# A hybrid HGRN2 / ConvFFN trunk: the order of the prologue written out, two more scale blocks on TensorE, and 32 bytes more of constants

## The chip, the cores and the metric

The kernel runs on one core of a Trainium2 chip. The metric is the time of one execution on the device in microseconds (us), the median of several runs. Beside the runs there is one profiled execution, of which every row below is taken. Engines are named as in the profile: PE is TensorE (PEld its weight loads), DVE VectorE, ACT ScalarE, POOL GpSimd, SP the queue that issues the transfers.

## The reference, cut to what matters

`DEPTH` is 1, so one layer runs: an HGRN2 mixer (8 heads, 2048 latent tokens behind 256 context tokens, width 1024) and a gated ConvFFN. What the change touches is the way into the mixer:

```python
m_l = (silu(c) @ w_ada + b_ada)          # six vectors of 1024: shift, scale, gate, ...
m_c = silu(c_ctx) @ w_ada + b_ada        # the same for the context tokens
hl = rmsnorm(lat, norm_g) * (1.0 + sc1) + sh1
hc = rmsnorm(cx,  norm_g) * (1.0 + csc1) + csh1
q, zf_fwd, zf_bwd, v, g = split(h @ w_in, 5)
f = lb + (1.0 - lb) * sigmoid(zf)        # forward and backward gates of the scan
```

`lb` comes from a softmax over two rows of logits.

## The kernel before

Everything runs with features on the partitions. The 2304 tokens are cut into units of 384 columns (`UN`), three token tiles each; the first unit holds the two context tiles and the first latent tile. For each unit a `Hidden` object makes the normed and modulated activations: `load` (one transfer to `xT`), `squares` (ACT, two halves), `sums` (four adds over the eight feature blocks), `scales` (a PE sum over partitions into `zs`, `rms_scale` with a power on POOL, a diagonal `dg`), `spread` (a PE matmul of `dg` with ones into `zr`, and two multiplications of `xT` by it on DVE), then per feature block k `high(k)` (ACT: scale and shift, then a rounded copy `hh`) and `low(k)` (DVE: the rest `hl = xT - hh`). A product is made of three fp32r matmuls, high by high, high by low and low by high (lines 337, 338, 339 for the first unit's gates; 488, 489, 490 elsewhere).

Before the loop over heads and units there is the prologue, `begin`. It makes SiLU(c), copies it along the partitions as rows `silrow` (a diagonal `dgs`, four PE matmuls, four ACT copies), and for each of the eight feature blocks j loads two blocks of `w_ada`: one for the shift and one for the scale. `by_pe(j, i)` multiplies a block with SiLU(c) on PE (eight fp32 matmuls; the trace shows each as two). For j under `NPE` = 3 the scale block goes that way too; for the others `by_dve(j)` makes two dot products on DVE (`junk`, line 320). The factors `B1` (shift) and `A1` (scale) were made on DVE, lines 327 and 328. `split_w0(ty)` rounds one 512 KB type of the first head's weights (`wh` or `vh`, ACT) and makes its rest (`wl` or `vl`). `gates(k)` adds feature block k to the first unit's two gate sums. Meanwhile the second unit's activations are begun; its sums, and the rest of one weight type, ran on POOL (`sums(pool)`, `split_w0(4, pool)`).

`begin` was recorded like all else, and the tile framework's scheduler set the order on each engine: it could also pull later work into the prologue, such as the products of the first unit's values (the 24 matmuls `z<-vh,hh` of 384 columns, lines 488 to 490) and the second unit's `high` and `low`. From then on the first unit goes on with `unit` (lines 523 and following), and the second unit's gates begin with the `z<-hh,wh` matmul behind the two transposes of line 656.

Constants lie at the bottom of the on-chip memory: `vec`, `ident`, `mhalf` (8 columns of -0.5, 32 bytes per partition), `ones` and so on; pools stacked on the left side follow them, other pools hang from the right side.

Of the kernel before, what the change touches and what calls it, by code (L numbers as in the profile page):

```python
# [9 lines left out]
F32 = mybir.dt.float32  # L10
# [3 lines left out]
AF = mybir.ActivationFunctionType  # L14
OP = mybir.AluOpType
# [4 lines left out]
D = 1024  # L20
# [3 lines left out]
KT = 8  # L24
# [18 lines left out]
UN = 384  # L43
NSC = 3
NS = 12
SEG = 33
NPE = 3


def body(ctx, tc, a, out):  # L50
# [18 lines left out]
    def small(name, shape=(128, 8), dt=F32):  # L69
        return cst.tile(list(shape), dt, name=name)  # L70

    mhalf = small("mhalf")
    pool.memset(mhalf, -0.5)

    def rms_scale(dst, ss, n, width):

        dve.tensor_scalar(dst, ss, 1.0 / width, EPS, OP.mult, OP.add)
        pool.tensor_tensor(dst, dst, mhalf[:, 0:n], OP.pow)
# [69 lines left out]
    class Hidden:  # L148
# [15 lines left out]
                ks = slice(g * 4, g * 4 + 4)  # L164
                act.activation(self.sq[:, ks], self.x[:, ks], AF.Square)

        def sums(self, e=dve):
            q = self.sq
            for i, j, n in ((0, 2, 2), (4, 6, 2), (0, 4, 2), (0, 1, 1)):
                e.tensor_tensor(q[:, i:i + n], q[:, i:i + n], q[:, j:j + n], OP.add)  # L170

        def scales(self):
            z = self.ps.tile([128, NSC, 2], F32, name="zs", tag="tr")
            for s in range(NSC):
                pe.matmul(z[:, s], self.sq[:, 0, s * 128:(s + 1) * 128], ones[:, 0:2],
                          start=True, stop=True)
            rs = self.xp.tile([128, NSC], F32, name="rsx", tag="rsx", bufs=2)
            rms_scale(rs, z[:, :, 0], NSC, D)
            self.dg = self.xp.tile([128, NSC, 128], F32, name="dg", tag="dg")
            diag(self.dg, rs)  # L180

        def spread(self):
            z = self.ps.tile([128, 1, UN], F32, name="zr", tag="tr")
            pe.matmul(z[:, 0], ones, self.dg.rearrange("p s n -> p (s n)"), start=True, stop=True)
            for g in range(2):
                x = self.x[:, g * 4:g * 4 + 4]
                dve.tensor_tensor(x, x, z.to_broadcast([128, 4, UN]), OP.mult)

        def modulate(self, k):
            for m, c in ((1, slice(0, self.nc)), (0, slice(self.nc, UN))):  # L190
# [19 lines left out]

        def steps(self):
            return [lambda: (self.load(), self.squares()), self.sums, self.scales,
                    self.spread] + self.pairs()

    def diag(dst, w):
        n = w.shape[-1]
# [26 lines left out]
    def begin(xp, ps):  # L243


        p0 = pool_(c0, "p0", side="right")
        act.activation(sil, vec[:, V_C:V_C + 16], AF.Sigmoid)
        dve.tensor_tensor(sil, sil, vec[:, V_C:V_C + 16], OP.mult)
        silv = sil.rearrange("p (two k) -> p k two", two=2)

        hid = [Hidden(u, u, xp, ps, x) for u, x in
               enumerate((place(5, [128, KT, UN], F32, "xT"), place(4, [128, KT, UN], F32, "xT"),
                          None))]
        w = head_tiles()
# [12 lines left out]
        def split_w0(ty, e=dve):
            wh, wl = type_parts(w, ty)
            raw = raws[ty].rearrange("p (k n) -> p k n", k=KT)
            act.activation(wh, raw, AF.Copy)  # L270
            e.tensor_tensor(wl, raw, wh.bitcast(F32), OP.subtract)

        hid[0].load()
        piece(0)
        piece(1)
        raw_w(1, 2)
        piece(2)
        hid[1].load()
        piece(3)
        piece(4)  # L280
        raw_w(0, 3, 4)
        for j in range(5, KT):
            piece(j)

        l0, l1 = vec[:, V_LB:V_LB + 16], vec[:, V_LB + 16:V_LB + 32]
        mx = p0.tile([128, 16], F32, name="mx")
        e2 = p0.tile([128, 2, 16], F32, name="e2")
        eb = p0.tile([128, 32], F32, name="eb")
        pool.memset(eb, float(np.e))
        bp = p0.tile([128, 8], F32, name="bp")  # L290
        acc = p0.tile([128, 2, 8], F32, name="dot")

        dgs = place(2, [128, 16, 128], F32, "dgs")
        silrow = xp.tile([128, 2, D], F32, name="silrow", tag="xT")
        for q in range(4):
            qs = slice(q * 4, q * 4 + 4)
            diag(dgs[:, qs], sil[:, qs])
            z = ps.tile([128, 512], F32, name="z", tag="sc", bufs=2)
            pe.matmul(z, ones, dgs[:, qs].rearrange("p s n -> p (s n)"), start=True, stop=True)
            act.activation(silrow[:, q // 2, q % 2 * 512:(q % 2 + 1) * 512], z, AF.Copy)  # L300
        dve.tensor_tensor(mx, l0, l1, OP.max)
        dve.tensor_tensor(e2[:, 0], l0, mx, OP.subtract)
        dve.tensor_tensor(e2[:, 1], l1, mx, OP.subtract)
        e2f = e2.rearrange("p a b -> p (a b)")
        pool.tensor_tensor(e2f, eb, e2f, OP.pow)
        dve.tensor_scalar(bp, vec[:, V_BA + 8:V_BA + 16], 1.0, None, OP.add)

        def by_pe(j, i):
            z = ps.tile([128, 2, 64], F32, name="z", tag="sc", bufs=2)
            b = blocks.pop((j, i)).rearrange("p (k n) -> p k n", k=KT)  # L310
            for k in range(KT):
                pe.matmul(z, b[:, k], silv[:, k, :, None].to_broadcast([128, 2, 64]),
                          start=k == 0, stop=k == KT - 1)
            return z[:, :, 0]

        def by_dve(j):
            b = blocks.pop((j, 1))
            for m in range(2):
                junk = xp.tile([128, D], F32, name="junk", tag="acc")
                dve.scalar_tensor_tensor(junk, b, 1.0, silrow[:, m], OP.mult, OP.mult,  # L320
                                         accum_out=acc[:, m, j:j + 1])
            return acc[:, :, j]

        def ada(j):
            shift = by_pe(j, 0)
            scale = by_pe(j, 1) if j < NPE else by_dve(j)
            dve.tensor_scalar(B1[:, :, j], shift, vec[:, V_BA + j:V_BA + j + 1], None, OP.add)
            dve.tensor_scalar(A1[:, :, j], scale, bp[:, j:j + 1], vec[:, V_NG + j:V_NG + j + 1],
                              OP.add, OP.mult)

        zs = [ps.tile([128, UN], F32, name="z", tag="pj", bufs=3) for _ in range(2)]

        def gates(k):
            h, l = part("h", 0)[:, k], part("l", 0)[:, k]
            for d in range(2):
                sh, sl = w[0][d]
                pe.matmul(zs[d], sh[:, k], h, start=k == 0, stop=False)
                pe.matmul(zs[d], sh[:, k], l, start=False, stop=False)
                pe.matmul(zs[d], sl[:, k], h, start=False, stop=k == KT - 1)

        high = lambda k: hid[0].high(slice(k, k + 1))
        low = lambda k: hid[0].low(slice(k, k + 1))

        hid[0].squares()
        hid[0].sums()
        dve.tensor_tensor(mx, e2[:, 0], e2[:, 1], OP.add)
        dve.reciprocal(mx, mx)
        dve.tensor_tensor(lb, e2[:, 0], mx, OP.mult)
        dve.tensor_tensor(oml, e2[:, 1], mx, OP.mult)
        ada(0)  # L350
        ada(1)
        hid[0].scales()
        split_w0(1)
        hid[0].spread()
        split_w0(2)
        high(0)
        high(1)
        low(0)
        ada(2)
        high(2)  # L360
        low(1)
        gates(0)
        ada(3)
        high(3)
        low(2)
        gates(1)
        hid[1].squares()
        hid[1].sums(pool)
        ada(4)
        high(4)  # L370
        low(3)
        gates(2)
        ada(5)
        high(5)
        low(4)
        gates(3)
        split_w0(0)
        split_w0(3)
        gates(4)
        ada(6)  # L380
        high(6)
        low(5)
        split_w0(4, pool)
        hid[1].scales()
        gates(5)
        ada(7)
        high(7)
        low(6)
        hid[1].spread()
        low(7)  # L390
        gates(6)
        gates(7)
# [27 lines left out]
    def mixer_scan():  # L420
        xp = pool_(c1, "xp", side="right")
        ps = pool_(c1, "ps", space=PSUM)
        head0, begun, hid = begin(xp, ps)
        c0.close()
        gp = pool_(c1, "gp", side="right")

# [1121 lines left out]
```

## Time and profile before

| what | value |
|---|---|
| three runs | 2859.32, 2859.48, 2864.54 us; median 2859.48 |
| the profiled execution | 2864.76 us, its span 2863.0 us, so 1.8 us lie outside of the span |
| PE busy | 2802.6 us, 98% of the span |
| DVE, ACT, POOL busy | 2093.5, 1151.4 and 610.4 us |
| mean granted TensorE clock | 0.992 |

How to read the rows: a timeline row gives the start (us), the duration (us), engine, line, operation, out<-in, shapes, how many were merged, and in brackets the idle time before and what ended it. A row of the windows gives for each stretch its length, then busy time and count by engine, the granted clock, the share of the transfer engines and GB/s. A row of the chain gives start, length, engine, tile and line.

### The profile page before, as it was taken

How to read it: one execution, taken by the hardware profiler on the slowest of the kernel's cores; microseconds unless marked ns; L12 is line 12 of the kernel's file. 1: busy time of each engine (PE TensorE's matmuls, PEld its weight loads, DVE VectorE, ACT ScalarE, POOL GpSimd, SP SyncE). 2: the span in 40 equal slices, each digit the busy share in tenths (PEclk: the TensorE clock that was granted, in tenths of full speed). 3: DMA queues.
4: the chain of work that ended last, by engine and by line, in shares of the span. 5: the costliest groups of instructions: out<-in, count | busy, mean ns of one | idle time of the engine just before them, and what ended most of it. 6: DMA issues, size and time to landing. Idle time of an engine off the chain costs nothing.

```text
span 2863.0 us, 42888 instructions
## 1 busy us (share of the span) xinstructions
PE 2802.6 (98%) x15768; PEld 2484.1 (87%) x15768; DVE 2093.5 (73%) x3486; ACT 1151.4 (40%) x2408; POOL 610.4 (21%) x1024
## 2 busy tenths in 40 slices
PE   7999999999999999999997999999999999999998
PEld 6999999999999999997886888888888888877887
DVE  7766666587566666578985888887877887576886
ACT  5433333354333333333555444444444444333343
POOL 4211111111111111111111534433434431000001
PEclk9999999999999999999998999999999999999999
DMA  5322222222222322236787322226222223987653
GB/s 236 104 79 71 91 91 64 78 86 70 81 84 71 107 90 66 78 105 240 292 304 291 128 89 74 89 89 263 90 87 76 88 89 125 306 289 242 198 181 118
DMA packets 201179, 386.51 MB, mean 135 GB/s; under 512 B 26500, under 2 KB 117636, under 8 KB 194952
## 3 DMA queue, kind: packets, MB, share of 16 engines
q1 hardware_dynamic: 199384, 379.70, 39.5%
q10 hardware_dynamic: 1584, 4.06, 0.4%
q8 instruction: 124, 2.03, 0.3%
q14 instruction: 87, 0.71, 0.1%
HBM read 281.70 MB, written 101.99 MB: 134 GB/s over the span
## 4 chain that ended last, share of the span: by engine, by line
PE 88%; DMA 4%; DVE 3%; ACT 2%; issue 1%; POOL 1%; SPq 0%; DVEq 0%; ACTq 0%; POOLq 0%
PE z L488 10%; PE z L490 10%; PE z L489 10%; PE y L1377 4%; PE y L1375 4%; PE y L1376 4%; PE zc L855 3%; PE zd L855 3%; PE zd L854 3%; PE zc L854 3%; PE zc L852 3%; PE zd L852 3%; PE za L855 3%; PE za L854 3%; PE za L852 3%; PE kv L699 2%
## 5 line engine op out<-in xcount | busy, mean ns | idle before, releaser
L488 PE MATMUL z<-vh,hh 128*128 128x256 f32 (+1 forms) x1024 | 299.8, 293 | 0.0
L490 PE MATMUL z<-vh,hl 128*128 128x256 f32 (+1 forms) x1024 | 293.2, 286 | 0.0
L489 PE MATMUL z<-vl,hh 128*128 128x256 f32 (+1 forms) x1024 | 293.0, 286 | 0.0
L488 PE MATMUL z<-hh,wh 128*128 128x384 f32 x752 | 257.3, 342 | 0.0
L490 PE MATMUL z<-hh,wl 128*128 128x384 f32 x752 | 252.1, 335 | 0.0
L489 PE MATMUL z<-hl,wh 128*128 128x384 f32 x752 | 252.0, 335 | 0.0
L1377 PE MATMUL y<-wd,ml 128*128 128x512 f32 x600 | 237.8, 396 | 1.9 <-DVE ml L82 1.9
L1375 PE MATMUL y<-wd,mh 128*128 128x512 f32 x600 | 237.4, 396 | 0.7 <-ACT X L1410 0.7
L1376 PE MATMUL y<-wd,mh 128*128 128x512 f32 x600 | 237.3, 396 | 0.0
L605 POOL COPY TX<-S 128x3 f32<-128x3 f32 x48 | 29.4, 614 | 805.4 <-DVE S L569 805.4
L488 PEld LDWEIGHTS z<-vh,hh 128*128 128x128 f32 x1024 | 196.1, 191 | 0.4 <-ACT vh L270 0.4
L489 PEld LDWEIGHTS z<-vl,hh 128*128 128x128 f32 x1024 | 195.8, 191 | 0.0
L490 PEld LDWEIGHTS z<-vh,hl 128*128 128x128 f32 x1024 | 195.5, 191 | 0.0
L82 DVE TENSOR_TENSOR w<-s,w 128x512 fp32r<-128x512 f32 x132 | 143.6, 1095 | 65.0 <-ACT w L81 64.6
L82 DVE TENSOR_TENSOR w<-raw,w 128x512 fp32r<-128x512 f32 x176 | 125.4, 715 | 43.5 <-ACT w L81 43.0
L81 ACT ACTIVATE w<-raw 128x512 fp32r<-128x512 f32 x176 | 108.9, 626 | 118.1 <-DMA raw<-in_w_up_dram 38.8
L545 DVE TENSOR_TENSOR st<-z,st 128x128 f32<-128x128 f32 x127 | 36.1, 287 | 157.8 <-ACT st L544 157.8
L1139 DVE SCALAR_TENSOR_TENSOR r<-uv,conv,r 128x1023 f32<-128x1023 f32 (+1 forms) x88 | 149.4, 1716 | 1.6 <-ACT r L1135 1.6
L488 PEld LDWEIGHTS z<-hh,wh 128*128 128x128 f32 x752 | 142.0, 189 | 3.5 <-DVE st L545 2.6
L540 ACT ACTIVATE v<-z 128x128 f32<-128x128 f32 x128 | 35.4, 277 | 269.7 <-PE z L490 269.7
L489 PEld LDWEIGHTS z<-hl,wh 128*128 128x128 f32 x752 | 141.8, 189 | 0.0
L490 PEld LDWEIGHTS z<-hh,wl 128*128 128x128 f32 x752 | 141.4, 188 | 0.0
(338 smaller groups left out, 8038.1 us busy)
## 6 DMA issues: line engine op xcount, KB each, us to landing
raw<-in_w_up_dram SPq DMA_DIRECT2D x90, 512.0 KB, 3.7
raw<-in_w_in_dram SPq DMA_DIRECT2D x75, 512.0 KB, 3.6
lr<-m SPq DMA_DIRECT2D x49, 512.0 KB, 5.9
m<-r SPq DMA_DIRECT2D x66, 256.0 KB, 3.7
raw<-in_w_ada_dram SPq DMA_DIRECT2D x32, 512.0 KB, 4.8
stash<-st SPq DMA_DIRECT2D x125, 128.0 KB, 1.8
kq<-stash SPq DMA_DIRECT2D x15, 1024.0 KB, 6.0
og<-stash SPq DMA_DIRECT2D x15, 1024.0 KB, 5.7
```

Of the source, the lines that this page charges most:

```text
L81: act.activation(h, src, AF.Copy)
L82: dve.tensor_tensor(l, src, h.bitcast(F32), OP.subtract)
L488: pe.matmul(o, sh[:, k], mh[:, k], start=k == 0, stop=False)
L489: pe.matmul(o, sh[:, k], ml[:, k], start=False, stop=False)
L490: pe.matmul(o, sl[:, k], mh[:, k], start=False, stop=k == KT - 1)
L852: pe.matmul(o, w[:, 0, k], r[:, :, 0, k], start=start and k == 0, stop=False, skip_group_check=True)
L854: pe.matmul(o, w[:, 0, k], r[:, :, 1, k], start=False, stop=False, skip_group_check=True)
L855: pe.matmul(o, w[:, 1, k], r[:, :, 0, k], start=False, stop=k == 3, skip_group_check=True)
L1139: dve.scalar_tensor_tensor(r, x, cw, r, OP.mult, OP.add)
L1375: pe.matmul(z, lh, rh, start=start, stop=False, skip_group_check=True)
L1376: pe.matmul(z, lh, rl, start=False, stop=False, skip_group_check=True)
L1377: pe.matmul(z, ll, rh, start=False, stop=stop, skip_group_check=True)
```

## The change

The order in `begin` is now the order in which the code is written, by a `manual_schedule` block around it, and the code was put in a new order for that. The second unit's sums and the rest of weight type 4 went from POOL to DVE; in the prologue POOL keeps three powers and the constants. `NPE` is 5: scale blocks 3 and 4 are multiplied on PE. `factors(j)` makes `B1` and `A1` on ACT, with `bp` now (1 + bias) times the norm's gain. The four `silrow` matmuls have a PSUM buffer each. The three transfers of the weight types 0, 3 and 4 come after all `ada` blocks. `mhalf` has 16 columns in place of 8.

```diff
-NPE = 3
+NPE = 5
...
-    mhalf = small("mhalf")
+    mhalf = small("mhalf", (128, 16))
...
-        dve.tensor_scalar(bp, vec[:, V_BA + 8:V_BA + 16], 1.0, None, OP.add)
+        ng = vec[:, V_NG:V_NG + 8]
+        dve.scalar_tensor_tensor(bp, vec[:, V_BA + 8:V_BA + 16], 1.0, ng, OP.add, OP.mult)
...
+        def factors(j):
+            act.activation(B1[:, :, j], zb[j], AF.Identity, bias=vec[:, V_BA + j:V_BA + j + 1])
+            act.activation(A1[:, :, j], za[j], AF.Identity, bias=bp[:, j:j + 1],
+                           scale=ng[:, j:j + 1])
...
+        h0.total()
+        h0.root()
+        ada(2)
+        h0.spread()
+        factors(2)
+        h0.scaled(0)
+        high_w(1)
+        high(0)
+        h0.scaled(1)
+        high_w(2)
+        low_w(1)
+        low_w(2)
+        high(1)
+        low(0)
...
+        ada(6)
+        h1.total()
+        h1.root()
+        dots(6)
+        low(5)
+        factors(6)
+        high(6)
+        gates(5)
+        ada(7)
+        h1.spread()
+        dots(7)
+        low(6)
+        factors(7)
+        high(7)
+        h1.scaled(0)
+        gates(6)
+        low(7)
+        gates(7)
+        h1.scaled(1)
+        for ty in (0, 3, 4):
+            high_w(ty)
+            low_w(ty)
...
-        head0, begun, hid = begin(xp, ps)
+        with tc.manual_schedule():
+            head0, begun, hid = begin(xp, ps)
```

`total` and `root` are the two halves of `scales`, `scaled(g)` one multiplication of `spread`, `high_w` and `low_w` the two halves of `split_w0`, `dots` the two dot products of `by_dve`.

The order on DVE in the second half of the prologue. Here `junk,dot` are the dot products, `hl` the rests (`hl_297` and `hl_319` both mean the first unit), `rsx`, `dg` and `xT<-xT,zr` the second unit's norm. Before:

```order
L271 TENSOR_TENSOR vl<-wada,vh 128x8x128 x2
L77 TENSOR_SCALAR rsx<-zs 128x3
L202 TENSOR_TENSOR hl_297<-xT,hh_292 128x384
L217 TENSOR_TENSOR dg<-ident,rsx 128x384
L320 SCALAR_TENSOR_TENSOR junk,dot<-wada,silrow 128x1024
L327 TENSOR_SCALAR B_108<-z,vec 128x2
L320 SCALAR_TENSOR_TENSOR junk,dot<-wada,silrow 128x1024
L187 TENSOR_TENSOR xT<-xT,zr 128x1536
L328 TENSOR_SCALAR A_107<-dot,bp,vec 128x2
```

The same place on DVE in the changed kernel, from the second unit's norm on:

```order
L77 TENSOR_SCALAR rsx<-zs 128x3
L225 TENSOR_TENSOR dg<-ident,rsx 128x384
L330 SCALAR_TENSOR_TENSOR junk,dot<-wada,silrow 128x1024 x2
L210 TENSOR_TENSOR hl_319<-xT,hh_310 128x384
L330 SCALAR_TENSOR_TENSOR junk,dot<-wada,silrow 128x1024 x2
L210 TENSOR_TENSOR hl_319<-xT,hh_310 128x384
L195 TENSOR_TENSOR xT<-xT,zr 128x1536
L210 TENSOR_TENSOR hl_319<-xT,hh_310 128x384
L195 TENSOR_TENSOR xT<-xT,zr 128x1536
L281 TENSOR_TENSOR vl<-wada,vh 128x8x128 x3
```

The factors have left DVE, the dot products for block 6 and the rest of block 5 stand behind the norm's `rsx` and `dg`, and the three `vl`, one of them POOL's before, stand last, behind the second unit's multiplications.

On PE at the end of the prologue the value products (`z<-vh,hh_292`, `z<-vl,hh_292`, `z<-vh,hl_297`) stood between the gates (`wh`, `wl`) before:

```order
L312 MATMUL z<-sil,wada 128x128 x8
L490 MATMUL z<-vh,hl_297 128x384
L337 MATMUL z<-hh_292,wh 128x384 x2
L488 MATMUL z<-vh,hh_292 128x384
L489 MATMUL z<-vl,hh_292 128x384
L490 MATMUL z<-vh,hl_297 128x384
```

In the changed kernel PE has at that place, from block 6 on:

```order
L322 MATMUL z<-sil,wada 128x128 x8
L179 MATMUL zs<-ones,sq 128x2 x3
L350 MATMUL z<-hh_310,wh 128x384
L351 MATMUL z<-hl_319,wh 128x384
L352 MATMUL z<-hh_310,wl 128x384
L350 MATMUL z<-hh_310,wh 128x384
L351 MATMUL z<-hl_319,wh 128x384
L352 MATMUL z<-hh_310,wl 128x384
L322 MATMUL z<-sil,wada 128x128 x8
L190 MATMUL zr<-dg,ones 128x384
```

All value products now stand behind the last gate. On ACT the start of the prologue was, before,

```order
L247 ACTIVATE sil<-vec 128x16
L165 ACTIVATE sq<-xT 128x1536 x2
L300 ACTIVATE silrow<-z 128x512 x4
L270 ACTIVATE wh<-wada 128x1024 x2
L165 ACTIVATE sq<-xT 128x1536
```

and is now

```order
L255 ACTIVATE sil<-vec 128x16
L309 ACTIVATE silrow<-z 128x512 x4
L165 ACTIVATE sq<-xT 128x1536 x2
L340 ACTIVATE B_108<-z,vec 128x2
L341 ACTIVATE A_107<-z,bp,vec 128x2
```

with the first unit's squares behind the four `silrow` copies. Behind the prologue the instructions of all engines stand in the order that they had. In memory the 32 bytes move the tiles of the left-side pools by 32 bytes (the weights `wh` and `vh`, the first unit's `hh` and `hl`, and in the FFN the weight tiles `w` and `wd`); those of the right side (`wada`, and in the FFN `rT`, `rB`, `mh`, `ml`) stay.

More of the change, by code (lines that the diff above doesn't have):

```diff
@@ L165, in squares, with sums, total @@
                 act.activation(self.sq[:, ks], self.x[:, ks], AF.Square)
-        def sums(self, e=dve):
+        def sums(self):
             q = self.sq
             for i, j, n in ((0, 2, 2), (4, 6, 2), (0, 4, 2), (0, 1, 1)):
-                e.tensor_tensor(q[:, i:i + n], q[:, i:i + n], q[:, j:j + n], OP.add)
+                dve.tensor_tensor(q[:, i:i + n], q[:, i:i + n], q[:, j:j + n], OP.add)
         def scales(self):
-            z = self.ps.tile([128, NSC, 2], F32, name="zs", tag="tr")
+            self.total()
+            self.root()
+        def total(self):
+            self.zs = z = self.ps.tile([128, NSC, 2], F32, name="zs", tag="tr")
             for s in range(NSC):
@@ L176, in scales, with root @@
                           start=True, stop=True)
+        def root(self):
             rs = self.xp.tile([128, NSC], F32, name="rsx", tag="rsx", bufs=2)
-            rms_scale(rs, z[:, :, 0], NSC, D)
+            rms_scale(rs, self.zs[:, :, 0], NSC, D)
             self.dg = self.xp.tile([128, NSC, 128], F32, name="dg", tag="dg")
@@ L184, in spread, with scaled @@
             pe.matmul(z[:, 0], ones, self.dg.rearrange("p s n -> p (s n)"), start=True, stop=True)
-            for g in range(2):
-                x = self.x[:, g * 4:g * 4 + 4]
-                dve.tensor_tensor(x, x, z.to_broadcast([128, 4, UN]), OP.mult)
+            self.z = z
+        def scaled(self, g):
+            x = self.x[:, g * 4:g * 4 + 4]
+            dve.tensor_tensor(x, x, self.z.to_broadcast([128, 4, UN]), OP.mult)
         def modulate(self, k):
@@ L212, in steps @@
             return [lambda: (self.load(), self.squares()), self.sums, self.scales,
-                    self.spread] + self.pairs()
+                    lambda: (self.spread(), self.scaled(0), self.scaled(1))] + self.pairs()
     def diag(dst, w):
@@ L265, in raw_w, with high_w, low_w @@
                 sp.dma_start(raws[ty], a["w_in"][0, ty])
-        def split_w0(ty, e=dve):
+        def high_w(ty):
+            raws[ty] = raws[ty].rearrange("p (k n) -> p k n", k=KT)
+            act.activation(type_parts(w, ty)[0], raws[ty], AF.Copy)
+        def low_w(ty):
             wh, wl = type_parts(w, ty)
-            raw = raws[ty].rearrange("p (k n) -> p k n", k=KT)
-            act.activation(wh, raw, AF.Copy)
-            e.tensor_tensor(wl, raw, wh.bitcast(F32), OP.subtract)
+            dve.tensor_tensor(wl, raws[ty], wh.bitcast(F32), OP.subtract)
         hid[0].load()
-        piece(0)
-        piece(1)
+        for j in range(3):
+            piece(j)
         raw_w(1, 2)
-        piece(2)
+        piece(3)
         hid[1].load()
-        piece(3)
-        piece(4)
+        for j in range(4, KT):
+            piece(j)
         raw_w(0, 3, 4)
-        for j in range(5, KT):
-            piece(j)
         l0, l1 = vec[:, V_LB:V_LB + 16], vec[:, V_LB + 16:V_LB + 32]
@@ L297, in begin @@
             diag(dgs[:, qs], sil[:, qs])
-            z = ps.tile([128, 512], F32, name="z", tag="sc", bufs=2)
+            z = ps.tile([128, 512], F32, name="z", tag=("pj", "pj", "pj", "o")[q],
+                        bufs=(3, 3, 3, 1)[q])
             pe.matmul(z, ones, dgs[:, qs].rearrange("p s n -> p (s n)"), start=True, stop=True)
@@ L314, in by_pe, with dots @@
             return z[:, :, 0]
-        def by_dve(j):
+        def dots(j):
             b = blocks.pop((j, 1))
@@ L321, in by_dve @@
                                          accum_out=acc[:, m, j:j + 1])
-            return acc[:, :, j]
+        zb, za = {}, {}
         def ada(j):
[L325 to L329, printed above, removed]
+            zb[j] = by_pe(j, 0)
+            za[j] = by_pe(j, 1) if j < NPE else acc[:, :, j]
+        def factors(j):
+            act.activation(B1[:, :, j], zb[j], AF.Identity, bias=vec[:, V_BA + j:V_BA + j + 1])
+            act.activation(A1[:, :, j], za[j], AF.Identity, bias=bp[:, j:j + 1],
+                           scale=ng[:, j:j + 1])
         zs = [ps.tile([128, UN], F32, name="z", tag="pj", bufs=3) for _ in range(2)]
@@ L342, in begin @@
         low = lambda k: hid[0].low(slice(k, k + 1))
-        hid[0].squares()
-        hid[0].sums()
+        h0, h1 = hid[:2]
+        h0.squares()
+        h0.sums()
         dve.tensor_tensor(mx, e2[:, 0], e2[:, 1], OP.add)
@@ L350, in begin @@
         ada(0)
+        factors(0)
         ada(1)
[L352 to L355, printed above, removed]
+        factors(1)
+        h0.total()
[5 more added lines that the diff above has]
+        high_w(1)
         high(0)
+        h0.scaled(1)
+        high_w(2)
+        low_w(1)
+        low_w(2)
         high(1)
         low(0)
-        ada(2)
         high(2)
         low(1)
-        gates(0)
+        low(2)
         ada(3)
+        factors(3)
         high(3)
[L365 to L368, printed above, removed]
+        h1.squares()
+        for k in range(3):
+            gates(k)
+        low(3)
+        h1.sums()
         ada(4)
+        factors(4)
         high(4)
-        low(3)
-        gates(2)
+        gates(3)
         ada(5)
+        dots(5)
+        factors(5)
         high(5)
         low(4)
-        gates(3)
-        split_w0(0)
-        split_w0(3)
         gates(4)
         ada(6)
+        h1.total()
[3 more added lines that the diff above has]
+        factors(6)
         high(6)
-        low(5)
-        split_w0(4, pool)
-        hid[1].scales()
         gates(5)
         ada(7)
+        h1.spread()
+        dots(7)
+        low(6)
+        factors(7)
         high(7)
-        low(6)
-        hid[1].spread()
+        h1.scaled(0)
+        gates(6)
         low(7)
-        gates(6)
         gates(7)
+        h1.scaled(1)
+        for ty in (0, 3, 4):
+            high_w(ty)
+            low_w(ty)
         return w, zs, hid
```

## The prediction

> **What bounds the kernel now.** I read the page, then busy time by stretch, then the waits and the chain of waits of the first 70 us, then the timeline there. First the page's head and its engine line, and the busy time by stretch (first PE, then PEld, DVE, ACT, POOL; of the last row PE alone):
>
> ```profile
> span 2863.0 us, 42888 instructions
> PE 2802.6 (98%) x15768; PEld 2484.1 (87%) x15768; DVE 2093.5 (73%) x3486; ACT 1151.4 (40%) x2408; POOL 610.4 (21%) x1024
> ...
> 0.00:70.00 70.00, 50.14 (x300) 41.50 (x301) 53.70 (x90) 37.92 (x61) 29.35 (x51) 0.95 0.61 241
> ...
> 70.00:100.00 30.00, 30.00 (x206) 29.24 (x205) 25.73 (x47) 13.53 (x32) 8.05 (x19) 1.00 0.10 24
> ...
> 100.00:560.00 460.00, 460.00 (x3256) 1.00 0.27 85
> ```
>
> PE is the bound, and idle for 2863.0 - 2802.6 = 60 us in all; 70 - 50.1 = 19.9 us of it lie in the first 70 us, and from there PE runs without a gap to 560 us. So whatever the prologue gains or loses is the shift of one event: the second unit's first gate matmul, which comes right behind the transposes of line 656. In the timeline it stands here:
>
> ```profile
> 64.09 0.34 PE L339 MATMUL z<-hh,wl 128*128 128x384 f32 x1
> ...
> 64.72 0.39 PE L488 MATMUL z<-hh,vh 128*128 128x256 f32 x1
> ...
> 67.68 0.28 PE L490 MATMUL z<-hh,vl 128*128 128x256 f32 x1
> 69.69 0.44 PE L656 MATMUL z<-ident,vt 128*128 128x128 f32 x2 [1.73 <-ACT vt L653]
> ...
> 70.14 0.34 PE L489 MATMUL z<-hl,wh 128*128 128x384 f32 x1
> ...
> 73.96 0.34 PE L490 MATMUL z<-hh,wl 128*128 128x384 f32 x1
> ```
>
> The gates end at 64.4, the transposes start at 69.69. The last two rows are the ends of 23 matmuls: (73.96 - 70.14) / 22 = 0.174 us from start to start at 384 columns; 64.72 to 67.68 holds 24 of 256 columns and a transpose, 0.119 each.
>
> What makes the prologue long is in the chain of waits: DVE and POOL rows that are far longer than their like. Two rows of the timeline show what ran beside the first two, and one the last:
>
> ```profile
> 23.84 2.15 DVE dg L217
> ...
> 36.84 2.07 DVE hl L202
> 38.92 1.96 DVE junk L320 x2
> ...
> 43.25 2.89 POOL vl L271
> ...
> 47.30 0.56 DVE dg L217
> ...
> 23.77 1.80 POOL L170 TENSOR_TENSOR sq<-sq 128x768 f32<-128x768 f32 x1
> ...
> 33.86 5.93 POOL L170 TENSOR_TENSOR sq<-sq 128x768 f32<-128x768 f32 x3 [8.29 <-ACT sq L165]
> 34.06 1.65 DVE L328 TENSOR_SCALAR A<-dot,bp,vec 128x2 f32<-128x2 f32 x1
> ...
> 40.93 0.27 DVE L328 TENSOR_SCALAR A<-dot,bp,vec 128x2 f32<-128x2 f32 x1
> 41.12 0.54 DVE L202 TENSOR_TENSOR hl<-xT,hh 128x384 fp32r<-128x384 f32 x1
> ...
> 43.93 2.62 DVE L202 TENSOR_TENSOR hl<-xT,hh 128x384 fp32r<-128x384 f32 x1
> ```
>
> Beside POOL's adds (23.77 on, 33.86 to 39.8) and its `vl` (43.25 to 46.14) DVE's rows are stretched: `dg` 2.15 for 0.56, `A` 1.65 for 0.27, `hl` 2.07 for 0.54 and 2.62 for 0.54, `junk` 1.96 for 1.22 (a row below). Together 1.59 + 1.38 + 1.53 + 2.08 + 0.74 = 7.3 us, nearly all of it on the chain.
>
> **The change, part by part.** Taking POOL out removes these 7.3 us. Against it stand more work on PE, a fixed order with waits of its own, and the loss of the fillers. I walk PE's new order with the durations of these rows (the first two by stretch, with the transfers' share and GB/s at the end):
>
> ```profile
> 0.00:20.00 20.00, 12.22 (x55) 7.86 (x56) 9.62 (x21) 8.41 (x10) 14.22 (x36) 0.91 0.91 358
> 20.00:40.00 20.00, 14.34 (x110) 13.47 (x110) 15.75 (x20) 10.24 (x16) 8.40 (x5) 1.00 0.99 405
> ...
> 4.27 3.68 PE L299 MATMUL z<-dgs,ones 128*128 128x512 f32 x4 [4.27 <-DVE dgs L217]
> ...
> 8.06 2.86 ACT L165 ACTIVATE sq<-xT 128x1536 f32<-128x1536 f32 x2 [5.06 <-DMA xT<-in_xt_dram]
> ...
> 11.46 3.49 PE L299 MATMUL z<-dgs,ones 128*128 128x512 f32 x4 [3.52 <-ACT silrow L300]
> ...
> 14.79 7.31 PE L312 MATMUL z<-sil,wada 128*128 128x128 f32 x64
> ...
> 22.94 0.86 POOL L78 TENSOR_TENSOR rsx<-rsx,mhalf 128x3 f32<-128x3 f32 x1 [6.34 <-DVE rsx L77]
> ...
> 26.13 0.88 PE L184 MATMUL zr<-dg,ones 128*128 128x384 f32 x2 [2.03 <-DVE dg L217]
> ...
> 27.05 3.42 DVE L187 TENSOR_TENSOR xT<-xT,zr 128x1536 f32<-128x1536 f32 x2 [1.07 <-PE zr L184]
> ...
> 41.59 2.35 DVE L271 TENSOR_TENSOR vl<-wada,vh 128x1024 fp32r<-128x1024 f32 x2
> ...
> 47.78 1.22 DVE L320 SCALAR_TENSOR_TENSOR junk<-wada,silrow 128x1024 f32<-128x1024 f32 x1
> ...
> 51.75 1.95 PE L312 MATMUL z<-sil,wada 128*128 128x128 f32 x16
> ```
>
> *Start.* PE's 3.5 us wait for `silrow` at 11.46 goes, since each matmul has its own PSUM buffer. The first pair ends at 7.8 as before; the second takes 3.5 us (the row, in a stretch whose clock was 0.91) down to half of it, if the clock is up by then, so the four end at 9.6 to 11.4, against 14.95; I take 10.4. The squares, now behind the copies, run from about 11.0 to 13.9, three us later than before; PE's four blocks (7.3 us) end at 17.7 and hide them and the adds. The sum over partitions (about 0.75) ends at 18.4, block 2 (two blocks, 3.9) at 22.3 with `rsx`, the power and `dg` beside it, the spread (0.88) at 23.2. That is 3.8 us earlier than before (26.13 + 0.88 = 27.0). The transfers keep up: two units (1.57 MB each), two weight types and the 16 blocks of `ada` (0.52 MB each) are 12.6 MB ahead of the last block of `ada`; by the two rows above 20 x 358 = 7.2 MB are there at 20 us and the rest 5.4 / 0.405 = 13 us later, at 33, while the walk below needs that block at 49. The three weight types moved last are needed last.
>
> *First gates.* DVE then does both multiplications (3.42), two `wl` (2.35) and one `hl` (0.54), to 29.5; PE, done with block 3 at 27.1, waits 2.2 us. Gates 0 to 2 (17 more matmuls by 0.174) end at 32.5, block 4 (shift and scale, 3.9) at 36.4, gates 3 at 37.5, block 5 at 39.4, gates 4 at 41.0 behind two dot products and an `hl`, block 6 at 43.0, the second unit's sum at 43.7.
>
> *Gates 5.* Their `hl` stands on DVE behind a wait: `rsx` waits for that PE sum, then power 0.86, `dg` 0.56, two dots 2.4, `hl` 0.54, with hand-overs 4.8 us. PE waits in order until 48.5, 4.6 us idle, where before it had value products to fill in. Gates 5 end at 49.4, block 7 at 51.3, the spread at 52.2, gates 6 at 53.2; gates 7 wait for one multiplication (1.75) and `hl`, 54.5, and end at 55.4: 9.0 us earlier than the 64.4 of before.
>
> *Given back.* All 24 value products of 384 columns are still to do (before, all but one stood ahead of 64.4), and three `vl` come on DVE behind another multiplication: 56.2, 57.4, 58.5, 59.7. PE has one product and two value matmuls of 256, then waits 2.7 us to 58.5. Ten by 0.119, 23 by 0.174, twelve by 0.119 and a transpose: 65.3. `vt` comes last on ACT, with a wait like the one at 69.69 but shorter, since the third unit's squares now stand behind it: I take 0.6, between 0 and 1.73. The transposes start at 66.0, 3.7 us earlier, at a full clock.
>
> *The clock.* Three consecutive stretches of 3.41 us (busy PE, PEld, DVE, ACT, POOL, then the clock):
>
> ```profile
> 38.42:41.84 3.42, 2.17 (x14) 2.09 (x15) 3.42 (x7) 1.36 (x3) 1.29 (x2) 1.00 0.33 134
> 41.84:45.25 3.41, 3.41 (x13) 2.96 (x14) 3.41 (x4) 1.75 (x3) 2.00 (x1) 0.50 0.01 2
> 45.25:48.66 3.41, 3.12 (x18) 2.37 (x18) 2.66 (x3) 0.00 (x0) 2.02 (x2) 1.00 0.00 0
> ```
>
> The first, with PE idle for more than a third of it, is followed by one at half clock, which costs up to 3.41 / 2 = 1.7 us. Before paid that once after the start. The new order has idle stretches of 2.2, 4.6 and 2.7 us; where the grid of stretches falls on them is chance. I take six in ten, certain and three in four, 2.35 x 1.7 = 4.0 us, and 0.7 for a second slow stretch behind the long one: +4.7. By the Trainium skill, "TensorE: Matmul & The Clock Gate", section "What's actually happening", the slow state needs at least one idle window of about 3.4 us; the first row here was busy for 2.17 of 3.42 us and was followed by 0.50 all the same. By that rule only the 4.6 us would slow the clock, and the clock term would be 1.7.
>
> *Edits with one answer.* The factors on ACT are sixteen small instructions ahead of the `high` that waits for them, as on DVE before; ACT is busy for 38 of 70 us. The two more blocks on PE (3.9 us) are in the walk; they take four dots (4 x 1.22 us) off DVE. POOL's 5.47 us power for `lb` comes later, and its readers only in the first unit's gates. The 32 bytes: FFN weights move to rows at an odd multiple of 32 bytes, where `rT` lies already, while `wd` lay at an even one:
>
> ```profile
> L1377 PE MATMUL y<-wd,ml 128*128 128x512 f32 x600 | 237.8, 396 | 1.9 <-DVE ml L82 1.9
> ...
> L852 PE MATMUL zc<-rT,w 128*128 128x512 f32 x352 | 139.0, 395 | 0.0
> ```
>
> 396 and 395 ns for the same shape: no cost, and 1 ns as bound either way.
>
> *Sum.* -3.7 + 4.7 = +1.0 us, bounds of the prologue -3.7 (never a slow stretch) to +4 (two behind each wait). The profiled execution took 2864.76, its median sister runs 2859.48, 5.3 less; I forecast 2865.8 profiled and **2860.5 us** as median. One change of 0.2% is 5.7 us, about what this measurement can tell from none (its three runs spread over 5.2).
>
> **Rivals.** *Slow stretches rarer:* only the 4.6 us wait slows the clock, -3.7 + 1.7 = -2.0, 2857.5 us. Against it speaks the first of the three stretches; for it that the waits of 2.2 and 2.7 may straddle two stretches. 18 in 100. (This is the case that the section of the Trainium skill named above would give.) *The stretched DVE rows come back whole:* the waits of the new order are shorter than walked, down to nothing at gates 5 and at `vl`, and the 7.3 us stay: 2852.2 us. For it: gates end 9 us earlier even in my walk. Against: the value products and `vl` have no other place. 13 in 100. *Slower, by the 32 bytes:* if operands at other rows cost PE 1 ns per matmul, 15768 of them make 15.8 us, 2876 us; it decides against "no change" from 0.36 ns (5.7 us / 15768) on. The two means above, 1 ns apart in the other direction, speak against it. 9 in 100. *No effect of the order itself* is not a case of its own: the order of the built program is as written.
>
> **How the numbers follow.** Forecast 60 in 100, own range 2857 to 2864; with the rarer slow stretches 78 in 100 lie within 0.2%. Faster by more 13, slower by more 9. The range 2854.0 to 2866.0 leaves out the faster and the slower rival and takes in the bounds -3.7 and +4 with about 2 us of run-to-run spread on either side.
>
> **What would show it.** POOL's adds gone from the first 70 us and no DVE row of 384 columns over 0.7 us; a PE wait of 4 to 5 us for `hl` near 44 to 49; a wait of two to three us on `vl` after the gates, which end near 55 to 60; half clock after it; the transposes behind the value products at 68 to 73. I am wrong if these start before 65 or after 75, if PE waits between them and 560, or if the mean of the 512-column matmuls moves off 395 to 396 ns.

## Result and profile after

The changed kernel takes 2829.74 us (median of 4 runs, 2826.41 to 2831.53) where the kernel before takes 2859.82 beside it: ratio 0.989, 95% interval 0.9873 to 0.9907. The prediction was 2860.5, its range 2854.0 to 2866.0: the time lies 24 us below the range. The prologue did nearly what was forecast; the 30 us came from the edit that the prediction costed at nothing, the 32 bytes.

The page's head and engine line of the changed kernel:

```profile
span 2828.4 us, 42949 instructions
PE 2770.4 (98%) x15800; PEld 2490.5 (88%) x15800; DVE 2080.5 (74%) x3467; ACT 1155.2 (41%) x2424; POOL 604.3 (21%) x1019
```

Busy time by stretch of the changed kernel: the first 70 us with all engines, the first 20 of them, and, with PE alone, 50 us of the FFN's up-projection and 50 of its down-projection (busy us, matmuls, clock, transfers' share, GB/s); in the second fence these two stretches of the kernel before:

```profile
0.00:70.00 70.00, 55.92 (x339) 49.97 (x340) 44.99 (x70) 41.25 (x77) 23.67 (x50) 0.90 0.61 242
...
0.00:20.00 20.00, 15.90 (x100) 12.68 (x101) 8.30 (x19) 8.02 (x13) 16.18 (x37) 1.00 0.91 358
...
1700.00:1750.00 50.00, 50.00 (x222) 1.00 0.27 84
...
2500.00:2550.00 50.00, 50.00 (x222) 1.00 0.87 298
```

```profile
1700.00:1750.00 50.00, 50.00 (x216) 1.00 0.21 64
...
2500.00:2550.00 50.00, 49.31 (x212) 1.00 0.86 291
```

PE is full in the FFN in both kernels (98.6% at least), at full clock, and still gets 222 matmuls through in 50 us where it got 216 and, with 0.69 us idle, 212. These counts take in the matmuls that run over either end of the stretch, so 50 / 222 = 0.225 us and 50 / 216 = 0.231 us are a little less than the distance from start to start, which is 0.227 us now and 0.234 us before. A busy share hides this, since a slower matmul is busy longer; the count beside it shows it.

The groups of the profile for matmuls of 512 columns, first of the changed kernel, then one row of the kernel before that the prediction had not quoted:

```profile
L1408 PE MATMUL y<-wd,mh 128*128 128x512 f32 x600 | 233.6, 389 | 0.1
...
L885 PE MATMUL zc<-rT,w 128*128 128x512 f32 x352 | 136.9, 389 | 0.0
...
L970 PE MATMUL y<-wo,gh 128*128 128x512 f32 x256 | 100.0, 391 | 0.0
```

```profile
L937 PE MATMUL y<-wo,gh 128*128 128x512 f32 x256 | 100.0, 391 | 0.0
```

In the FFN the mean fell from 395 and 396 ns to 389. In the output projection of the mixer (`wo`) it was 391 before and is 391 after. So a matmul of this shape had already been quicker in one stage of the kernel before. (The length of a matmul in these rows overlaps the next one; what PE pays is the distance from start to start, and that is used from here on. By the starts in the traces it is 234 ns in the FFN before, 227 after, and 227 in the `wo` rows of both; a median over each group.)

Going along PE's starts, the changed kernel is 1.2 us ahead at the transposes behind the second unit's gates, 0.9 at the FFN's first matmul (at 1534 us in the changed kernel), 25.1 at the first of the down-projection (at 2395 us) and 35.7 at its last. The medians differ by 30: the profiled execution of before took 2864.8, 4.9 above the median beside it.

### The profile page after: what moved, and what is told of

It reads as the page before. It is cut to its first block, busy times and chain, and to the rows that moved or that the text cites. A ratio compares the mean times of both kernels' runs of the same rounds, so it can differ in the third digit from the quotient of the medians.

```text
span 2828.4 us, 42949 instructions
## 1 busy us (share of the span) xinstructions
PE 2770.4 (98%) x15800; PEld 2490.5 (88%) x15800; DVE 2080.5 (74%) x3467; ACT 1155.2 (41%) x2424; POOL 604.3 (21%) x1019
## 4 chain that ended last, share of the span: by engine, by line
PE 79%; DVE 8%; DMA 7%; issue 2%; ACT 1%; POOL 1%; SPq 0%; DVEq 0%; POOLq 0%; ACTq 0%
PE z L523 11%; PE z L521 11%; PE z L522 11%; PE zd L888 3%; PE zd L885 3%; PE zd L887 3%; PE zc L888 3%; PE zc L885 3%; PE zc L887 3%; PE za L888 3%; PE za L885 3%; PE za L887 3%; PE kv L732 2%; DMA lr<-m 2%; PE sc L715 2%
## 5 line engine op out<-in xcount | busy, mean ns | idle before, releaser
L1408 PE MATMUL y<-wd,mh 128*128 128x512 f32 x600 | 233.6, 389 | 0.1
L1409 PE MATMUL y<-wd,mh 128*128 128x512 f32 x600 | 233.5, 389 | 0.0
```

Source lines behind the costliest of these rows:

```text
L1408: pe.matmul(z, lh, rh, start=start, stop=False, skip_group_check=True)
L1409: pe.matmul(z, lh, rl, start=False, stop=False, skip_group_check=True)
```

## Experiments

The stationary operand of a matmul is the one that its weight load (PEld) reads, the moving operand is the other. Addresses below are those of the tiles in the built programs; the traces hold none. What counts turned out to be the distance from PE's moving operand to its stationary one, modulo 256 bytes. In the FFN before, `w` and `wd` lie at 64 modulo 256 and `rB`, `rT`, `mh`, `ml` at 96: 32 apart. In the changed kernel all lie at 96. In the output projection `wo`, `gh` and `gl` lie together at 64 before and at 96 after; in the mixer's projections `hh`, `hl`, `wh`, `wl`, `vh`, `vl` lie together as well, in both kernels.

### The shift alone, and the order alone

```diff
-    mhalf = small("mhalf")
+    mhalf = small("mhalf", (128, 16))
```

in the kernel before, and the reverse in the changed kernel.

> The kernel before with nothing but the 32 bytes: the constant of the powers has 16 columns in place of 8, and with it all tiles of SBUF's left side lie 32 bytes higher, those of the right side where they were. Theory (a 512-column matmul takes 227 ns from start to start where its moving and its stationary operand lie at the same offset modulo 64 bytes, 234 where they differ by 32): all 5448 matmuls of the FFN go from 234 to 227 ns, 5448 x 6.6 ns = -36 us, so about 2824 to 2829 us, with the prologue as before. Rival (the new order of the prologue, and what it sets off later, brought the time): 2859 us, 234 ns.

> The changed kernel without the 32 bytes (the constant has 8 columns again): order, work on PE and ScalarE's factors as changed. Theory of the offset: 234 ns in the FFN, the transposes behind the second unit's gates near 68.5 as in the changed kernel, 1 to 3 us below the kernel before, 2857 to 2860 us. Rival of the order: 2830 us.

The shift alone: 2831.75 us against 2862.55, ratio 0.9889 (0.9872 to 0.9905). The order alone: 2861.43, ratio 0.9995 (0.9986 to 1.0005). The same stretches, first with the shift alone, then with the order alone:

```profile
1700.00:1750.00 50.00, 50.00 (x222) 1.00 0.21 65
```

```profile
1700.00:1750.00 50.00, 50.00 (x216) 1.00 0.21 64
```

The whole gain is the shift's; the new order, the work moved to PE and ScalarE's factors are worth about 1 us, which the interval does not tell from nothing. (The shift's 31 us are less than the 36 of its sum; what was given back is told below.) The rival that the new order brought the time fell.

### Which address matters: one operand of some matmuls

```diff
+    pool.memset(pool_(fr, "padr", side="right").tile([128, 8], F32, name="pad"), 0.0)
     rp = pool_(fr, "rp", side="right")
```

> The kernel before with 32 bytes put on the right side ahead of the pool of rT (and a small memset of them): rT1 to rT4 now lie at an even multiple of 32 bytes like w; rB11 to rB22, mh, ml and the whole left side stay. Theory of the relative offset: the 2112 matmuls that read rT go to 227 ns (2112 x 6.6 = -14 us, about 2845), those of rB and of the down-projection stay at 234. Rival (a row at an odd multiple of 32 bytes is the better one, for either operand): no matmul gets faster, 2859 us, or those of rT get slower. Rival (the rows of w alone matter, against the writes that ScalarE and VectorE make there): 2859 us.

2851.46 us, ratio 0.9959 (0.9944 to 0.9973): -11 us, where the sum had 14. Rows of this kernel:

```profile
L854 PE MATMUL zc<-rT,w 128*128 128x512 f32 x352 | 136.9, 389 | 0.0
...
L854 PE MATMUL za<-rB,w 128*128 128x512 f32 x336 | 132.6, 395 | 0.0
...
L1376 PE MATMUL y<-wd,mh 128*128 128x512 f32 x600 | 237.3, 396 | 0.0
```

Only the matmuls of `rT` got faster, in one run, on the same line of the code, beside the same engines: 227.4 ns from start to start in the mean, those of `rB` and `wd` 233. `rT` went to an even multiple of 32 bytes and `w` did not move: neither "the odd row is the better one" nor "the rows of `w` alone" can say that.

```diff
-    conv = h2p.tile([128, V_CN + 96], F32, name="conv")
+    conv = h2p.tile([128, V_CN + 104], F32, name="conv")
```

> The changed kernel, and 32 bytes on the right side too: rB, rT, mh and ml go from an odd to an even multiple of 32, while w and wd stay at the odd one, so all operands of the FFN are 32 bytes apart again, the other way round. Theory of the relative offset: 227 goes back to 234 ns and the gain is lost, about 2860 us. Rival (an odd row of the weights w and wd is what counts): 227 ns, 2829 us.

2859.9 us, ratio 0.9995 (0.9985 to 1.0004): the gain is gone, with `w` and `wd` at the same rows as in the changed kernel.

```profile
L888 PE MATMUL zc<-rT,w 128*128 128x512 f32 x352 | 139.2, 396 | 0.0
...
L1408 PE MATMUL y<-wd,mh 128*128 128x512 f32 x600 | 237.0, 395 | 0.0
```

### The period

The constant of the kernel before with 32, 48 and 80 columns in place of 8, all else as before:

```diff
-    mhalf = small("mhalf")
+    mhalf = small("mhalf", (128, 32))    # 48, 80
```

> The kernel before with a constant of 32 columns: the left side lies 96 bytes higher, so the operands of the FFN differ by 64 bytes modulo 128. If the period is 64 bytes: 227 ns and about 2824 to 2829 us, as with 32 bytes. If it is 128 or more (only equal offsets are good): 234 ns, 2859 us.

> The kernel before with a constant of 48 columns: the left side lies 160 bytes higher, so that the operands of the FFN differ by 128 bytes modulo 256, where the shift of 32 makes them equal modulo 256 and the shift of 96, which gained nothing, makes them differ by 64. If the period is 128 bytes: 227 ns, 2829 us. If it is 256 or more: 230 to 235 ns, 2845 to 2862 us.

> The kernel before with a constant of 80 columns: the left side lies 288 bytes higher. The operands of the FFN are then equal modulo 512, where the shift of 32 bytes left them 256 apart. If 256 bytes are the period (equal modulo 256 is good, shifts of 96 and 160 gained next to nothing): 227 ns and about 2829 us. If the period is 512 and 256 apart the good place: 231 to 235 ns, 2855 to 2861 us.

Shift of 96: 2861.37 us, 0.9993 (0.9984 to 1.0002). Of 160: 2860.82, 1.0001 (0.9992 to 1.0011). Of 288: 2834.45, 0.9906 (0.9889 to 0.9922). So 64 and 128 bytes apart gain nothing, 0 and 256 do; with the sections of TensorE alone below, which come again from 256 on, the period is 256. The three matmuls of the down-projection and one of the up-projection with the shift of 96, then one with that of 288:

```profile
L1377 PE MATMUL y<-wd,ml 128*128 128x512 f32 x600 | 236.9, 395 | 1.4 <-DVE ml L82 1.4
L1376 PE MATMUL y<-wd,mh 128*128 128x512 f32 x600 | 235.2, 392 | 0.0
L1375 PE MATMUL y<-wd,mh 128*128 128x512 f32 x600 | 232.9, 388 | 0.0
...
L852 PE MATMUL zc<-rT,w 128*128 128x512 f32 x352 | 139.2, 396 | 0.0
```

```profile
L852 PE MATMUL zc<-rT,w 128*128 128x512 f32 x352 | 136.9, 389 | 0.0
```

The shift of 96 makes the stationary operand lie 64 bytes ahead of the moving one in the up-projection and 64 behind it in the down-projection. The two are not alike: 395, 392 and 388 ns in the down-projection, 396 in the up-projection, or 229 and 233 ns from start to start in the mean. The sign of the distance counts too. The whole kernel's time hides this: in its one trace the FFN is 9 us shorter than in that of before (4 us shorter than with the order alone), but the way from the first transposes to the FFN is 6 us longer (1470.7 against 1465.1 us), and why is not shown.

```diff
-        w = p.tile([128, 2, 4, 128], F32R, name="w", tag=tag, bufs=bufs)
+        if tag == "w":
+            w = p.tile([128, 1040], F32R, name="w", tag=tag, bufs=bufs)
+            w = w[:, 4:1028].rearrange("p (a k n) -> p a k n", a=2, k=4)
...
```

and the like for `wd`:

> The kernel before with each w and wd of the FFN starting 16 bytes into a tile that is 64 bytes longer: the operands of the FFN are 16 bytes apart in place of 32. If the cost grows with the distance: about 230 ns, half of the gain, 2845 us. If any difference costs the whole: 234 ns, 2860 us. If differences within 32 bytes cost nothing: 227 ns, 2829 us.

2852.38 us, 0.9973 (0.9961 to 0.9984). The edit was badly made: a tile of 1040 columns is 4160 bytes, so each of the eleven ring buffers lies another 64 bytes further modulo 256, and the distance runs through four values. It can't tell its cases apart by itself. The table of the next run fits it in the up-projection: for `w` the distances are 240, 48, 112 and 176, which give (227.1 + 233.3 + 233.1 + 229.8) / 4 = 230.8 ns; its trace has 230.9 for `rT` and 231.0 for `rB` as mean from start to start (distances over 260 ns left out here and below). In the down-projection the distances are 16, 208, 144 and 80, for which the table has 231.4 and the trace 232.7.

### TensorE alone

A kernel of its own in place of the reference's work, in one execution: one PSUM bank per distance, 48 matmuls each, in the order (w0, m0), (w0, m1), (w1, m0).

```python
    def section(name, cols, mb, wb, count):
        z = ps.tile([128, 512], F32, name=name, tag="z")
        ws = [w[:, k * 256 + wb // 4:k * 256 + wb // 4 + 128] for k in range(2)]
        ms = [m[:, k * 512 + mb // 4:k * 512 + mb // 4 + cols] for k in range(2)]
        for i in range(count):
            k = i % 3
            pe.matmul(z[:, 0:cols], ws[k == 2], ms[k == 1], start=i == 0, stop=i == count - 1)
        act.activation(res[:, done[0]:done[0] + 1], z[:, 0:1], AF.Copy)
        done[0] += 1
```

> The disputed cost by itself: TensorE alone, no other engine at work and no transfers, 48 matmuls (two stationary and two moving tiles in turn, in the FFN's order) for each distance between stationary and moving operand. a: 512 columns, the stationary 0 to 496 bytes further, in steps of 16; b: the same in steps of 32 with the moving operand 32 bytes further; c: 256 columns; d: 384 columns. The reference's work is left out. Theory (a matter of the two operands alone): 227 ns in a at 0 and 256, 231 to 235 elsewhere, the same curve in b moved by 32 bytes; at 256 columns about 120 ns at 0 and 117 at 32, at 384 columns 173 to 174 everywhere, as the whole kernels showed. Rival (it needs the writes of ScalarE, VectorE or the transfers beside it): one value for all distances in each part.

PE's timeline of this kernel, start and length of each section (a000x: 512 columns, stationary 0 bytes further; b032x: both 32 bytes further; c: 256 columns):

```profile
19.59 11.04 PE L71 MATMUL a000x<-m,w 128*128 128x512 f32 x48
30.47 11.05 PE L71 MATMUL a016x<-m,w 128*128 128x512 f32 x48
41.36 11.35 PE L71 MATMUL a032x<-m,w 128*128 128x512 f32 x48
52.55 11.36 PE L71 MATMUL a048x<-m,w 128*128 128x512 f32 x48
...
375.25 11.37 PE L71 MATMUL b000x<-m,w 128*128 128x512 f32 x48
386.45 11.08 PE L71 MATMUL b032x<-m,w 128*128 128x512 f32 x48
397.37 11.35 PE L71 MATMUL b064x<-m,w 128*128 128x512 f32 x48
...
553.42 5.91 PE L71 MATMUL c000x<-m,w 128*128 128x256 f32 x48
559.17 5.84 PE L71 MATMUL c032x<-m,w 128*128 128x256 f32 x48
564.84 5.82 PE L71 MATMUL c064x<-m,w 128*128 128x256 f32 x48
```

From start to start of two sections, divided by 48: (30.47 - 19.59) / 48 = 226.7 ns with equal addresses, (52.55 - 41.36) / 48 = 233.1 at 32 bytes; b, with the moving operand 32 bytes further, has 233.3 at 0 and 227.5 at 32. All sections in the same way, in ns by distance of the stationary operand from the moving one; from 256 on the values come again within 0.5 (the starts are given to 0.01 us, which is 0.2 ns here):

| distance | 512 columns | 384 | 256 |
|---|---|---|---|
| 0 | 226.7 | 173.5 | 119.8 |
| 16 | 226.9 | | |
| 32 | 233.1 | 173.3 | 118.1 |
| 48 | 233.3 | | |
| 64 | 233.1 | 174.8 | 117.9 |
| 80 | 231.9 | | |
| 96 | 234.2 | 176.5 | 117.3 |
| 112 | 233.1 | | |
| 128 | 233.3 | 176.3 | 118.5 |
| 144 | 233.5 | | |
| 160 | 233.1 | 176.5 | 119.8 |
| 176 | 229.8 | | |
| 192 | 229.0 | 173.5 | 117.7 |
| 208 | 233.3 | | |
| 224 | 233.3 | 176.5 | 118.1 |
| 240 | 227.1 | | |

No other engine touches the operands while the sections run (ScalarE takes one column out of each finished bank), and next to nothing is transferred, so the cost is one between TensorE's own two operands; the rival that needs other traffic fell. The table gives every FFN row seen so far to about 1.5 ns: 0 (227), 32 and 224 (233), 192 against 64 for the two halves of the shift of 96 (229 and 233), and 128, where the shift of 160 has 232.3 in place of 233.3. The Trainium skill, "TensorE: Matmul & The Clock Gate", section "Wait — 56ns, not 53.3ns?", gives 215.7 ns from start to start at 512 columns. No distance here reached it: the lowest was 226.7, with a weight load for each matmul.

### The mixer: the rule does not carry over to other widths

```diff
+    pool.memset(pool_(c1, "padw").tile([128, 8], F32, name="pad"), 0.0)
     wp = pool_(c1, "wp", 2)
```

> The kernel before with 32 bytes put ahead of the mixer's weight pool: wh, wl, vh, vl (and hh of the third unit of each three) lie 32 bytes higher, hh and hl of the first two units and hl of the third do not; the FFN is as before. Theory (moving and stationary operand apart by 32 bytes cost 6.6 ns in each matmul of these forms): of some 6500 matmuls of 384 and 256 columns seven in nine go from 174 and 120 ns to 180 and 126, 5060 x 6.6 ns = +33 us, 2893 to 2896 us; the rest keeps its time. Rival (it costs only matmuls of 512 columns): 2860 us, 174 and 120 ns. Rival (the higher row is the better one): faster.

2856.29 us, ratio 0.9981 (0.9972 to 0.9991): faster by 5 us, where my theory said 33 slower and the rival nothing. Rows before, then of this kernel:

```profile
L488 PE MATMUL z<-vh,hh 128*128 128x256 f32 x960 | 277.4, 289 | 0.0
...
L488 PE MATMUL z<-hh,wh 128*128 128x384 f32 x752 | 257.3, 342 | 0.0
```

```profile
L489 PE MATMUL z<-vh,hh 128*128 128x256 f32 x960 | 274.2, 286 | 0.0
...
L489 PE MATMUL z<-hh,wh 128*128 128x384 f32 x752 | 259.0, 344 | 0.0
```

At 256 columns being 32 bytes apart helps. From start to start these matmuls take about 118 ns in place of 120, as in the table (`hh` lies 32 behind `vh`, distance 224: 118.1); those of 384 keep their 173 to 174. "Equal addresses are best" is a fact of 512 columns only, and my price per matmul had been carried from one width to another.

### Both at once

```diff
+    pool.memset(pool_(c1, "padw").tile([128, 8], F32, name="pad"), 0.0)
     wp = pool_(c1, "wp", 2)
+    pool.memset(pool_(c1, "padq").tile([128, 56], F32, name="pad"), 0.0)
     hq = pool_(c1, "hq")
```

in the changed kernel: 32 bytes, and 224 more to bring everything behind it back to where it lay modulo 256.

> The changed kernel with 32 bytes ahead of the mixer's weight pool and 224 bytes ahead of the pool behind it: in the FFN the operands stay equal modulo 256, in the mixer weights and hidden units are 32 bytes apart for all units. By the curve measured alone: 384 columns 173.3 ns as with equal offsets, 256 columns 117.8 to 118.3 in place of 120.0, so 2880 matmuls of 256 columns x about 2 ns = -5 to -6 us against the changed kernel, 2823 to 2826 us where the changed kernel has 2830; FFN 227 ns. If the curve measured alone does not hold beside the other engines: as the changed kernel.

> The changed kernel once more beside it: 2830 us, 227 ns in the FFN, 120 ns at 256 columns.

2820.65 us, ratio 0.9863 (0.9849 to 0.9878), beside the changed kernel's 2828.82 (0.9888, 0.9872 to 0.9905). The runs of the two do not overlap (2818.92 to 2824.78, 2827.55 to 2829.98): some 8 us faster than the changed kernel, 2 more than the upper end of what was expected.

```profile
L523 PE MATMUL z<-vh,hh 128*128 128x256 f32 x960 | 274.4, 286 | 0.0
```

In the two traces the way from the first transposes to the FFN's first matmul is 7.4 us shorter (1456.7 us, 1464.1 in the changed kernel); 2880 matmuls of 256 columns by 2 ns are 5.8 of them. In these traces they are closer by more than that: 2.7 to 3.2 ns from start to start by line, 8.5 us in all, so that some 1 us was given back elsewhere. The 2 ns of the table were too little for this place.

## Why the prediction was wrong, by its steps

**The step that failed: "the 32 bytes, no cost, 1 ns as bound either way".** They were worth -6.6 ns for each of some 5450 matmuls, -36 us. The two rows that I compared, `wd` with `ml` and `rT` with `w`, have in common what mattered: their operands lie 32 bytes apart, the one way and the other, and both take 233 ns from start to start. I looked at the address of the moving operand alone. Two rows of the same case bounded nothing. The sign of being wrong that the prediction named, a mean that moves off 395 to 396 ns, is the one that came: 389. The row that would have shown the price stood in the profile of before, `wo` with `gh`: same shape, operands at the same offset, 391 ns. The rival "slower, by the 32 bytes" had the right term, a cost of the address in each matmul, but the wrong sign, 1 ns where 6.6 were at stake, and all matmuls of the kernel in place of the FFN's; a fall was excluded without a reason.

**What was given back.** 36 us of matmuls became 30 in the medians. The FFN's faster PE runs into DVE: these two rows are the third matmul of the down-projection, with the order alone (234 ns) and with the shift alone (227); behind the last bar stands the idle time ahead of them:

```profile
L1410 PE MATMUL y<-wd,ml 128*128 128x512 f32 x600 | 237.3, 396 | 0.0
```

```profile
L1377 PE MATMUL y<-wd,ml 128*128 128x512 f32 x600 | 234.4, 391 | 4.4 <-DVE ml L82 4.2
```

Counting all distances above 260 ns between two starts in the FFN: 15 with 24.6 us with the order alone, 38 with 36.1 us in the changed kernel. Less the 227 ns that each of the 23 would take anyway, that is +6.3 us. The profiled execution of before had such waits too (35 distances, 34.1 us), which fits that the profiled pair differs by 34.8 us in the FFN and the medians by 30. The other traces bear it out, without an experiment on DVE's work: the five with 227 ns in the whole FFN have 37 to 39 such distances with 36 to 38 us, 16 to 20 of them in the down-projection; the down-projections at 233 ns have none in three traces (order alone, 32 bytes on the right side too, the mixer apart), 2 with `rT` moved, and 11 in that of before.

**The prologue, right to about 2 us.** PE's timeline of the changed kernel at the places of the walk:

```profile
4.09 5.59 PE L308 MATMUL z<-dgs,ones 128*128 128x512 f32 x8 [4.09 <-DVE dgs L225]
...
16.93 0.73 PE L179 MATMUL zs<-ones,sq 128*128 128x2 f32 x6
...
21.18 0.81 PE L190 MATMUL zr<-dg,ones 128*128 128x384 f32 x2
...
28.24 0.57 PE L351 MATMUL z<-hl,wh 128*128 128x384 f32 x1 [2.33 <-DVE hl L210]
...
42.22 0.73 PE L179 MATMUL zs<-ones,sq 128*128 128x2 f32 x6
...
47.60 0.69 PE L351 MATMUL z<-hl,wh 128*128 128x384 f32 x1 [4.38 <-DVE hl L210]
...
57.76 0.44 PE L521 MATMUL z<-vh,hh 128*128 128x384 f32 x1 [0.95 <-ACT vh L277]
...
59.61 0.58 PE L523 MATMUL z<-hh,vl 128*128 128x256 f32 x1 [0.97 <-DVE vl L281]
...
68.45 0.44 PE L689 MATMUL z<-ident,vt 128*128 128x128 f32 x2 [0.54 <-ACT vt L686]
```

| step of the walk | forecast | measured |
|---|---|---|
| `silrow` matmuls end | 10.4 | 9.7 |
| sum over partitions ends | 18.4 | 17.7 |
| spread ends | 23.2 | 22.0 |
| first `hl` matmul, PE's wait | 29.5, 2.2 | 28.2, 2.3 |
| second unit's sum ends | 43.7 | 43.0 |
| gates 5, PE's wait | 48.5, 4.6 | 47.6, 4.4 |
| gates end | 55.4 | 56.8 |
| first `vl` matmul; PE's waits ahead of it | 58.5; 2.7 | 59.6; 0.95 + 0.97 |
| transposes; wait on `vt` | 66.0 at full clock, 68 to 73 with the clock term; 0.6 | 68.45; 0.54 |

The walk was about 1 us late from 10 us to 48 us, 0.7 of it from the start on, where PE was at full clock (1.00 in the first 20 us, 0.91 before). From the end of the gates on it was early by 1 to 1.5 us: PE ran at half clock from 45.5 to 52.3 us, which the walk left to the clock term. The wait on `vl` came in two parts, the first on ScalarE's `vh`. The transposes stand at 69.7 to 71.7 us in the eight traces with the old order and at 68.4 to 69.5 in the five with the new one, so the order did gain about a microsecond there. DVE's rows of the same work lost their stretch, as forecast: `dg` 0.56 and `hl` 0.55.

```profile
18.84 0.56 DVE L225 TENSOR_TENSOR dg<-ident,rsx 128x384 f32<-128x384 f32 x1 [0.98 <-POOL rsx L78]
...
47.00 0.55 DVE L210 TENSOR_TENSOR hl<-xT,hh 128x384 fp32r<-128x384 f32 x1
```

**The clock term, right in kind, a little high.** Busy time by stretch around the three waits (PE, PEld, DVE, ACT, POOL, then the clock):

```profile
25.00:28.41 3.41, 1.08 (x8) 0.73 (x7) 3.41 (x5) 3.38 (x7) 0.00 (x0) 1.00 1.03 420
28.41:31.82 3.41, 3.41 (x12) 3.41 (x13) 1.36 (x3) 3.31 (x8) 0.00 (x0) 0.50 1.03 420
...
45.49:48.90 3.41, 1.29 (x4) 1.30 (x5) 3.34 (x8) 1.72 (x4) 0.00 (x0) 0.50 0.00 0
48.90:52.31 3.41, 3.41 (x17) 3.41 (x16) 1.54 (x3) 0.18 (x1) 0.00 (x0) 0.50 0.38 97
55.70:59.10 3.40, 1.99 (x8) 1.28 (x8) 3.40 (x3) 3.40 (x6) 0.00 (x0) 1.00 0.02 8
59.10:62.50 3.40, 2.89 (x12) 2.89 (x13) 3.40 (x6) 3.40 (x7) 0.00 (x0) 0.50 0.00 0
```

Each of the three waits was followed by half clock, the long one by two stretches. PE was busy for 3.41 + 1.29 + 3.41 + 2.89 = 11.0 us there, so 5.5 us of its work were lost, of which the transposes show 68.45 - 66.0 = 2.5, or 3.5 where the walk's own 1 us is taken off. That the rest fell into waits that grew shorter for it would fit the wait ahead of `vl` (1.9 us for 2.7), but is not shown. The forecast had 4.7. So the rival of rarer slow stretches fell, although its price, -2.0, is nearer to the -1.1 of the order alone than the forecast's +1.0: the term was too high by 1 to 2 us. The Trainium skill, "TensorE: Matmul & The Clock Gate", section "What's actually happening", asks for an idle window of about 3.4 us; here a stretch with PE busy for 1.99 of 3.40 us was followed by half clock (55.70 on), so the trace does not agree. But the one row that the prediction built its chances on was no rule either: in the trace of before, on the same grid of 3.41 us, stretches with PE busy for 2.05 us (from 24.77), 2.01 (28.18), 1.74 (35.01) and 1.86 (58.90) were followed by full clock, and the one with 2.17 by half. What decides is not shown. The slow stretches of the new order do come again: from 15 to 70 us its five traces have a mean clock of 0.84 to 0.91, the eight with the old order 0.89 to 0.97. The rival that the 7.3 us of stretched DVE rows come back whole fell too.

## What to carry to other kernels

An edit that moves tiles has a price of its own: before costing an edit at nothing, compare the addresses of both operands of the costliest matmuls, modulo 256 bytes here, before and after, and look in the profile for the same shape at another distance. A busy share near 100% says nothing on the rate; count matmuls in equal stretches, or measure from start to start. Which distance is good depends on the columns, so measure it at each width, and when PE gets faster, look for the operand that it now waits for.

## What was unexpected in the hardware

With fp32r operands and a weight load for each matmul, TensorE's rate depends on where its moving and its stationary operand lie in SBUF against one another, modulo 256 bytes: at 512 columns 226.7 to 227.1 ns within 16 bytes of equal and up to 234.2 elsewhere, at 384 columns 173.3 to 176.5, at 256 columns 117.3 to 119.8 with equal addresses among the worst. It needs no other engine. No run shows how the two operands meet: the mechanism inside stays open.
